# One encoder block on one core: the triangular inversion's rows move to PSUM, the key sums to ScalarE, and other units run beside the inversions

## The chip, the cores and the metric

The kernel runs on one core of a Trainium2 chip. The metric is the device time of one execution in microseconds (us). One execution of each kernel was also taken by the hardware profiler; all rows of a trace shown here are from such an execution.

The engines by their names in the profile: PE is TensorE's matmuls and PEld its weight loads, DVE is VectorE, ACT is ScalarE, POOL is GpSimd, SP is SyncE, which here only issues transfers.

## What is computed

One layer of an encoder for 512 positions and 1024 channels, all in float32:

```python
h = rmsnorm(x, norm1_w)
p, q, k, v, z, bf, bb, af, ab, g_pool, g_dn = split(h @ w_in)
y_pool = (multiscale_pool(p) @ pool_w * pool_scale) @ pool_out      # 4 window widths
q, k, v = split(silu(dwconv_centered([q, k, v], qkv_conv_w)))       # 5 taps along positions
q, k = l2norm(q) * 128 ** -0.5, l2norm(k)                           # 8 heads of 128 channels
o = delta(q, k, v, g_f, beta_f) + flip(delta(flip(q), flip(k), flip(v), flip(g_b), flip(beta_b)))
y_dn = (rmsnorm(o) * dn_norm_w * silu(z)) @ dn_out
x = x + (sigmoid(g_pool) * y_pool + sigmoid(g_dn) * y_dn) @ w_o
u = dwconv_centered(rmsnorm(x, norm2_w) @ ffn_up, ffn_conv_w, ffn_conv_b)
x = x + (silu(u_gate) * u_val) @ ffn_down
return rmsnorm(x, final_norm_w)
```

`delta` is the chunked gated delta rule: within a chunk it solves a system with the matrix I + L, where L is strictly lower triangular and holds the masked and decayed products of the chunk's keys. The kernel inverts such matrices instead.

## The kernel before

**Projections.** Every projection is a `job` (line 405): for 128 output channels and all 512 positions it multiplies 8 blocks of the contraction, each by three matmuls of 128x512 (`mm3`, lines 367 to 370), since weights and activations are split into a high and a low part. A job's weights are loaded raw (`wr_`, SP), cast to the high part by ScalarE (`wh_`, line 392) and subtracted to the low part by GpSimd (`wl_`, line 396). Its result is in a PSUM bank named `ps_`.

**What the units do behind it.** A q, k or v unit runs the convolution: ScalarE does the centre tap (line 736), VectorE four more taps that read PSUM (line 742), ScalarE the activation (752 for v, 754 for q and k). A z unit and a gate unit (`gd`, `gp`) need one ScalarE operation and a store to DRAM. A k unit goes on (`k_unit`): it transposes the keys to token order (line 766, `pt_k`), copies them (`ktok`), squares the other order (`ksq`, line 790), sums the squares by four matmuls with a column of ones (`kss`, line 795) and derives scales from them (798 to 802).

**The inversion.** There are two groups of four heads. For each head `mats_unit` multiplies the keys with themselves (the Gram products `pk`, line 830) and masks them (`nm`, line 837), and stores the 32x32 blocks on the diagonal to DRAM. `inv_unit` then loads a group's 128 blocks, one per partition and 1024 elements each, into SBUF (`rw`, and `un`, half of which ScalarE fills transposed, line 880). In 30 steps VectorE forms an outer product (`tmp`, line 887) and adds it to the rows below (`un`, line 891), both 30 to 240 elements per partition. Then ScalarE writes a transposed copy (`rv`, line 909) and four transfers bring `un` and `rv` to DRAM, from where `ext` is loaded. `merge_unit` builds the 64x64 inverses from there by matmuls (`l1a`, line 951, is the first), and `delta_unit` runs the recurrence for two heads, `fin_unit` normalises and gates the output.

**What sets the order.** The program calls the units one after the other (lines 1404 to 1461), and each adds tasks with an engine, a price in us, what it reads and writes, and a key. The `Planner` (lines 38 to 184) then lays them out in time by these prices: an engine that is free takes the ready task with the lowest key, when a buffer of its ring is free. The outcome is a fixed queue for each engine, worked off strictly in order. Keys of jobs count up in the order of the calls, so this order says which projection fills TensorE beside which chain. The rings (`RINGS`, line 242) are the numbers of buffers, with `oo` the two PSUM banks of the recurrence's output.

Beside the first inversion stand q and v of heads 0 and 1 and k of heads 4 to 7; beside the second q and v of heads 4 to 7 and z of 4 to 7. The gates `gd` come with the merges and recurrences.

Of the kernel before, what the change touches and what calls it, by code (L numbers as in the profile page):

```python
# [208 lines left out]
def hybrid_block(  # L209
# [561 lines left out]
    def k_unit(h, halves=False):  # L771
# [14 lines left out]
        b = {}  # L786

        def square():
            b["sq"] = ring("dp", "f", (P, S), F32, f"ksq_{h}")
            act.activation(b["sq"], kT[h], AF.Square)  # L790

        def sums():
            b["ps"] = bank("ds", f"kss_{h}")
            for t in range(NT):
                pe.matmul(b["ps"][:, t : t + 1], b["sq"][:, t * P : (t + 1) * P], ones[:, 0:1], start=True, stop=True)

        def norm():
            dve.tensor_scalar(out=kss[:, h, :], in0=b["ps"][:, 0:4], scalar1=L2_EPS, scalar2=None, op0=ALU.add)
# [57 lines left out]
    def inv_unit(g):  # L856
        c = CHAIN + 1000 * g + 400
        b = {}
        ui = CHAIN + 1000 * g + 500 - 1e6 * 0
# [4 lines left out]
        fl = lambda t_: t_.rearrange("u r c -> u (r c)")  # L864

        def open_un():
            b["un"] = ring("dp", "x4", (P, B32, B32), F32, f"un_{g}")

        Z(open_un, r=["pool:dp"], w=[f"x4:un{g}"], key=c)

        def load(d):
            if d == 0:
                b["rw"] = ring("dp", "x4", (P, B32, B32), F32, f"rw_{g}")
                sp.dma_start(fl(b["rw"][0:64]), blocks(b_scr[g], 0))
            else:
                sp.dma_start(fl(b["un"][64:128]), blocks(b_scr[g], 1))

        L(256, lambda: load(0), r=[f"bscr{g}", "pool:dp"], w=[f"x4:rw{g}"], key=c)
        L(256, lambda: load(1), r=[f"bscr{g}", "pool:dp"], w=[f"x4:un{g}#b"], key=c)
        A(1.1, lambda: act.copy(b["un"][0:64], b["rw"][0:64].rearrange("p r c -> p c r")),  # L880
          r=[f"x4:rw{g}"], w=[f"x4:un{g}#a"], key=c)

        def step(k):
            un = b["un"]
            n = B32 - 1 - k
# [1 line left out]
            dve.tensor_tensor(  # L887
                out=tm, in0=un[:, k + 1 :, k : k + 1].to_broadcast([P, n, k]),
                in1=un[:, k : k + 1, 0:k].to_broadcast([P, n, k]), op=ALU.mult,
            )  # L890
            dve.tensor_tensor(out=un[:, k + 1 :, 0:k], in0=un[:, k + 1 :, 0:k], in1=tm, op=ALU.add)  # L891
# [12 lines left out]

        V(0.1, end, w=[f"x4:un{g}"], key=c)

        def flip():
# [1 line left out]
            act.copy(b["rv"], b["un"].rearrange("p r c -> p c r"))
# [908 lines left out]
```

## Time and profile before

| what | us |
|---|---|
| median of 3 runs (971.36 to 973.51) | 972.35 |
| the profiled execution | 971.58 |
| its span, first to last recorded instruction | 969.9 |

The page cuts the span into 40 slices of 24.2 us. Each digit is the busy share of a slice in tenths, and PEclk is TensorE's granted clock in tenths of full speed:

```profile
PE   6999969999987889999999999999999999999997
DVE  4787994356689514457213514444344434400302
ACT  5586435244752322444344433444434444421323
POOL 3335234134753421558546860444444545444460
PEclk9999889999998989999999999999999999999999
```

Two places in the first half are less busy on PE (slice 6, and slices 12 to 15), and PEclk is lower there too. The page also follows the chain that ended last back from the last instruction, by engine:

```profile
PE 80%; DVE 12%; ACT 3%; DMA 2%; issue 2%; SPq 1%; POOL 1%; DVEq 0%; POOLq 0%; ACTq 0%
```

In the prediction, a row "start, duration, engine, line, operation, out<-in" is from the timeline, and `[8.52 <-DVE kss L798]` there is the engine's idle time before it and the instruction that ended it. A table of stretches gives for each engine the busy time and the number of instructions in that stretch, then the granted clock and the share of the DMA engines.

### The profile page before, as it was taken

The numbers are of one execution on the slowest core, as the hardware profiler recorded it, in microseconds if no ns is written. First come the engines' busy times: TensorE is split into PE (matmuls) and PEld (weight loads), VectorE is DVE, ScalarE is ACT, GpSimd is POOL, SyncE is SP. The second block draws the span as 40 slices with busy tenths as digits, with TensorE's granted clock in tenths as the row PEclk, the third lists the DMA queues.
The fourth block names the chain that finished last, engine by engine and source line by source line (L and its number), as shares of the span: only waits on it lengthen the run. The fifth ranks groups of instructions, "written<-read, shape, count | busy, mean of one in ns | idle before, by whom it ended". The sixth has DMA issues, their size and how long they took to land.

```text
span 969.9 us, 13976 instructions
## 1 busy us (share of the span) xinstructions
PE 924.5 (95%) x5362; PEld 772.7 (80%) x5362; DVE 457.8 (47%) x860; ACT 411.2 (42%) x646; POOL 428.5 (44%) x415
## 2 busy tenths in 40 slices
PE   6999969999987889999999999999999999999997
PEld 5878757888875669887788888888888888888886
DVE  4787994356689514457213514444344434400302
ACT  5586435244752322444344433444434444421323
POOL 3335234134753421558546860444444545444460
PEclk9999889999998989999999999999999999999999
DMA  6224225323332361323388740233323333222322
GB/s 203 77 72 102 66 73 126 86 77 87 99 91 62 96 167 34 112 65 103 97 268 299 267 152 2 88 107 88 109 87 107 88 104 92 97 100 90 107 87 87
DMA packets 162036, 104.76 MB, mean 108 GB/s; under 512 B 31365, under 2 KB 142770, under 8 KB 161970
## 3 DMA queue, kind: packets, MB, share of 16 engines
q1 hardware_dynamic: 161394, 102.82, 36.3%
q8 instruction: 42, 0.69, 0.3%
q10 hardware_dynamic: 576, 1.05, 0.3%
q14 instruction: 24, 0.20, 0.1%
HBM read 90.22 MB, written 13.63 MB: 107 GB/s over the span
## 4 chain that ended last, share of the span: by engine, by line
PE 80%; DVE 12%; ACT 3%; DMA 2%; issue 2%; SPq 1%; POOL 1%; DVEq 0%; POOLq 0%; ACTq 0%
PE ps_up L369 8%; PE ps_up L370 8%; PE ps_up L368 8%; PE dn L369 4%; PE dn L368 4%; PE dn L370 4%; DVE tmp L887 3%; DVE un L891 3%; PE ps_gd L368 2%; PE ps_z L368 2%; PE o L1164 2%; PE ps_wo L370 2%; PE ps_wo L368 2%; PE ps_wo L369 2%; PE ps_do L368 2%
## 5 line engine op out<-in xcount | busy, mean ns | idle before, releaser
L396 POOL TENSOR_TENSOR wl_up<-wr_up,wh_up 128x512 fp32r<-128x512 f32 x88 | 111.8, 1291 | 156.0 <-ACT wh_up L392 155.9
L369 PE MATMUL ps_up<-h_lo,wh_up 128*128 128x512 f32 (+1 forms) x368 | 139.9, 380 | 0.3 <-DVE h_lo L542 0.3
L368 PE MATMUL ps_up<-h_hi,wh_up 128*128 128x512 f32 (+1 forms) x368 | 140.0, 380 | 0.0
L370 PE MATMUL ps_up<-h_hi,wl_up 128*128 128x512 f32 (+1 forms) x368 | 139.8, 380 | 0.0
L1618 DVE SCALAR_TENSOR_TENSOR c<-ps_up,fw,c 128x511 f32<-128x511 f32 x88 | 66.0, 750 | 122.5 <-ACT c L1612 116.7
L369 PEld LDWEIGHTS ps_up<-h_lo,wh_up 128*128 128x128 f32 x368 | 69.2, 188 | 13.8 <-DVE h_lo L542 0.5
L368 PEld LDWEIGHTS ps_up<-h_hi,wh_up 128*128 128x128 f32 x368 | 69.2, 188 | 13.3
L370 PEld LDWEIGHTS ps_up<-h_hi,wl_up 128*128 128x128 f32 x368 | 69.2, 188 | 12.9
L396 POOL TENSOR_TENSOR wl_dn<-wr_dn,wh_dn 128x512 fp32r<-128x512 f32 x36 | 46.3, 1306 | 49.8 <-ACT wh_dn L392 49.8
L392 ACT CAST wh_up<-wr_up 128x1024 fp32r<-128x1024 f32 x44 | 46.3, 1053 | 47.5 <-PE ps_up L369 37.7
L369 PE MATMUL dn<-wl_dn,a 128*128 128x512 f32 (+1 forms) x158 | 58.6, 371 | 0.0
L368 PE MATMUL dn<-wh_dn,a 128*128 128x512 f32 (+1 forms) x158 | 58.6, 371 | 0.0
L370 PE MATMUL dn<-wh_dn,a 128*128 128x512 f32 (+1 forms) x158 | 58.5, 370 | 0.0
L1677 DVE TENSOR_TENSOR x<-dn,x 128x512 f32<-128x512 f32 (+1 forms) x9 | 5.7, 632 | 96.2 <-PE dn L370 96.1
L396 POOL TENSOR_TENSOR wl_gd<-wr_gd,wh_gd 128x512 fp32r<-128x512 f32 x16 | 20.2, 1281 | 64.7 <-ACT wh_gd L392 31.4
L392 ACT CAST wh_dn<-wr_dn 128x1024 fp32r<-128x1024 f32 x18 | 18.9, 1050 | 61.9 <-PE dn L370 60.1
L1640 ACT CAST a<-c 128x512 fp32r<-128x512 f32 x22 | 13.7, 621 | 53.8 <-DVE c L1636 53.8
L396 POOL TENSOR_TENSOR wl_q<-wr_q,wh_q 128x512 fp32r<-128x512 f32 x16 | 20.7, 1315 | 34.6 <-ACT wh_q L392 34.6
L368 PEld LDWEIGHTS dn<-wh_dn,a 128*128 128x128 f32 x158 | 29.8, 188 | 5.3
L370 PEld LDWEIGHTS dn<-wh_dn,a 128*128 128x128 f32 x158 | 29.7, 188 | 5.2
L369 PEld LDWEIGHTS dn<-wl_dn,a 128*128 128x128 f32 x158 | 29.8, 188 | 5.1
L1612 ACT ACTIVATE c<-ps_up,fw 128x512 f32<-128x512 f32 x44 | 33.8, 768 | 0.0
(334 smaller groups left out, 2410.7 us busy)
## 6 DMA issues: line engine op xcount, KB each, us to landing
wr_up<-in_ffn_up_dram SPq DMA_DIRECT2D x44, 512.0 KB, 3.9
wr_dn<-in_ffn_down_dram SPq DMA_DIRECT2D x22, 512.0 KB, 3.5
x<-in_x_dram SPq DMA_DIRECT2D x8, 512.0 KB, 7.5
wr_k<-in_w_in_dram SPq DMA_DIRECT2D x8, 512.0 KB, 4.0
wr_q<-in_w_in_dram SPq DMA_DIRECT2D x8, 512.0 KB, 4.0
wr_v<-in_w_in_dram SPq DMA_DIRECT2D x8, 512.0 KB, 3.8
wr_z<-in_w_in_dram SPq DMA_DIRECT2D x8, 512.0 KB, 3.9
wr_gd<-in_w_in_dram SPq DMA_DIRECT2D x8, 512.0 KB, 6.2
```

The source lines that it names most:

```text
L368: pe.matmul(ps, ahi, bhi, start=first, stop=False)
L369: pe.matmul(ps, ahi, blo, start=False, stop=False)
L370: pe.matmul(ps, alo, bhi, start=False, stop=last)
L392: act.copy(b["hi"], b["raw"])
L396: pool.tensor_tensor(out=b["lo"][:, sl], in0=b["raw"][:, sl], in1=f32(b["hi"][:, sl]), op=ALU.subtract)
L887: dve.tensor_tensor(out=tm, in0=un[:, k + 1 :, k : k + 1].to_broadcast([P, n, k]), in1=un[:, k : k + 1, 0:k].to_broadcast([P, n, k]), op=A ...
L891: dve.tensor_tensor(out=un[:, k + 1 :, 0:k], in0=un[:, k + 1 :, 0:k], in1=tm, op=ALU.add)
L1164: pe.matmul(o_ps[hh][:, ts(t)], st["w1"][:, s % 2, c, :], dts[hh][:, d, t, :], start=(s == 0 and d == 0), stop=(s == 3 and d == 1),)
L1612: act.activation(b[j], box["ps"], AF.Identity, scale=fw[:, 1, ci : ci + 1], bias=fw[:, 3, ci : ci + 1])
L1618: dve.scalar_tensor_tensor(out=y[:, lo:hi], in0=box["ps"][:, lo + sh : hi + sh], scalar=fw[:, k, ci : ci + 1], in1=y[:, lo:hi], op0=ALU.mu ...
L1640: act.copy(a_hl[c][:, 0, :], b[0])
L1677: dve.tensor_tensor(out=x2[t][:, c0:c1], in0=acc[hf, t, i][:, 0 : c1 - c0], in1=x2[t][:, c0:c1], op=ALU.add)
```

## The change

It has five parts.

1. `inv_unit`: the rows that the steps change, `un`, lie in PSUM, in one tile of two banks (`banks2`; the ring `oo` is now one such tile, which the recurrence's outputs use later). The input block `n` stays in SBUF as one factor of the outer product. ScalarE copies `n` to `un` (`take`) and, at the end, `un` back to SBUF twice, straight (`inv`) and transposed (`rev`), for the four stores.
2. `k_unit`: the squares and their sums are formed by ScalarE in one operation for each of a head's four token blocks, with its accumulator (`accum_out`), from `ktok`; the squares themselves go into the bank of the transposes. The squaring of `kT`, the four matmuls and a PSUM bank go.
3. The prices of GpSimd's copies and of the inversion's steps in the planner.
4. The order of units: beside the first inversion run z of all heads, q and v of heads 0 to 3 and four gates; beside the second q and v of heads 4 to 7, four gates `gd` and three `gp`. The keys of heads 4 to 7 come after the first recurrence. The pool units `p` and the other `gp` come beside the last recurrences.
5. Names in tasks that go with these (`oo`, the bank pairs of the last projection).

```diff
 def cp(n):
-    return 0.25 + n * 0.0024
+    return 0.17 + n * 0.0023
...
-        "pp": 3, "ds": 3, "oo": 2, "raw": 3, "whi": 2, "wlo": 2, "y": 5, "f": 5, "z": 2, "q": 4, "v": 4,
+        "pp": 3, "ds": 3, "oo": 1, "raw": 3, "whi": 2, "wlo": 2, "y": 5, "f": 5, "z": 2, "q": 4, "v": 4,
...
+
+    def banks2(name, shape=(P, 2, 512)):
+        return psum.tile(list(shape), F32, tag="oo", bufs=RINGS["oo"], name=name)
...
-        b = {}
-
-        def square():
-            b["sq"] = ring("dp", "f", (P, S), F32, f"ksq_{h}")
-            act.activation(b["sq"], kT[h], AF.Square)
-
         def sums():
-            b["ps"] = bank("ds", f"kss_{h}")
             for t in range(NT):
-                pe.matmul(b["ps"][:, t : t + 1], b["sq"][:, t * P : (t + 1) * P], ones[:, 0:1], start=True, stop=True)
+                act.activation(
+                    tb["pt"][:, t * P : (t + 1) * P], ktok[h][:, t, :], AF.Square, accum_out=kss[:, h, t : t + 1]
+                )
 
         def norm():
-            dve.tensor_scalar(out=kss[:, h, :], in0=b["ps"][:, 0:4], scalar1=L2_EPS, scalar2=None, op0=ALU.add)
+            dve.tensor_scalar(out=kss[:, h, :], in0=kss[:, h, :], scalar1=L2_EPS, scalar2=None, op0=ALU.add)
             dve.reciprocal(rk2[:, h, :], kss[:, h, :])
             for d in range(2):
                 dve.tensor_tensor(out=bp[:, :, h, d], in0=beta[:, :, h, d], in1=rk2[:, h, rev(d)], op=ALU.mult)
             dve.tensor_scalar(out=nbp[:, :, h, :], in0=bp[:, :, h, :], scalar1=-1.0, scalar2=None, op0=ALU.mult)
 
-        A(ca(512), square, r=[f"kT{h}", "pool:dp"], w=[f"f:ksq{h}"], key=c)
-        M(0.5, sums, r=[f"f:ksq{h}"], w=[f"ds:kss{h}"], key=c)
-        V(0.45, norm, r=[f"ds:kss{h}", "beta"], w=[f"ks{h}"], key=c)
         A(ca(512), keep, r=[tn], w=[f"kk{h}"], key=c)
+        A(2.2, sums, r=[f"kk{h}"], w=[tn, f"ks{h}"], key=c)
+        V(0.85, norm, r=["beta"], w=[f"ks{h}"], key=c)
...
+        Z(lambda: b.update(n=block("n")), r=["pool:dp"], w=[f"x4:n{g}"], key=c)
+        Z(lambda: b.update(rw=block("rw")), r=["pool:dp"], w=[f"x4:rw{g}"], key=c)
+        L(256, lambda: sp.dma_start(fl(b["rw"][lo_]), blocks(b_scr[g], 0)), r=[f"bscr{g}"], w=[f"x4:rw{g}"], key=c)
+        L(256, lambda: sp.dma_start(fl(b["n"][hi_]), blocks(b_scr[g], 1)), r=[f"bscr{g}"], w=[f"x4:n{g}#1"], key=c)
+        A(1.1, lambda: act.copy(b["n"][lo_], b["rw"][lo_].rearrange("p r c -> p c r")),
+          r=[f"x4:rw{g}"], w=[f"x4:n{g}#0"], key=c)
+
+        def take():
+            b["un"] = banks2(f"un_{g}", (P, B32, B32))
+            act.copy(b["un"], b["n"])
+
+        A(1.1, take, r=[f"x4:n{g}"], w=[f"oo:un{g}"], key=c)
...
         def step(k):
             un = b["un"]
             n = B32 - 1 - k
+            if k == 1:
+                b["tmp"] = ring("dp", "x2", (P, 256), F32, f"tmp_{g}")
             tm = b["tmp"][:, 0 : n * k].rearrange("p (r c) -> p r c", c=k)
             dve.tensor_tensor(
-                out=tm, in0=un[:, k + 1 :, k : k + 1].to_broadcast([P, n, k]),
+                out=tm, in0=b["n"][:, k + 1 :, k : k + 1].to_broadcast([P, n, k]),
                 in1=un[:, k : k + 1, 0:k].to_broadcast([P, n, k]), op=ALU.mult,
             )
             dve.tensor_tensor(out=un[:, k + 1 :, 0:k], in0=un[:, k + 1 :, 0:k], in1=tm, op=ALU.add)
 
...
-        def first(k):
-            b["tmp"] = ring("dp", "x2", (P, 256), F32, f"tmp_{g}")
-            step(k)
-
         for k in range(1, B32 - 1):
-            V(0.16 + 2 * (B32 - 1 - k) * k / 960.0, lambda k=k: (first if k == 1 else step)(k),
-              r=[], w=[f"x4:un{g}", f"x2:tmp{g}"], key=c)
+            V(0.44 + 2 * 0.00105 * (B32 - 1 - k) * k, lambda k=k: step(k),
+              r=[f"x4:n{g}"], w=[f"oo:un{g}", f"x2:tmp{g}"], key=c)
 
         def end():
-            un = b["un"]
-            dve.memset(un.rearrange("p r c -> p (r c)")[:, 0 : B32 * B32 : B32 + 1], 1.0)
...
-        V(0.1, end, w=[f"x4:un{g}"], key=c)
-
-        def flip():
-            b["rv"] = ring("dp", "x4", (P, B32, B32), F32, f"rv_{g}")
-            act.copy(b["rv"], b["un"].rearrange("p r c -> p c r"))
-
-        A(1.1, flip, r=[f"x4:un{g}"], w=[f"x4:rv{g}"], key=c)
-        hi_, lo_ = slice(64, 128), slice(0, 64)
-        L(256, lambda: sp.dma_start(blocks(u_scr[g], 1), fl(b["un"][hi_])), r=[f"x4:un{g}"], w=[f"uscr{g}#1"], key=c)
-        L(256, lambda: sp.dma_start(blocks(e_scr[g], 0), fl(b["un"][lo_])), r=[f"x4:un{g}"], w=[f"escr{g}#0"], key=c)
-        L(256, lambda: sp.dma_start(blocks(u_scr[g], 0), fl(b["rv"][lo_])), r=[f"x4:rv{g}"], w=[f"uscr{g}#0"], key=c)
-        L(256, lambda: sp.dma_start(blocks(e_scr[g], 1), fl(b["rv"][hi_])), r=[f"x4:rv{g}"], w=[f"escr{g}#1"], key=c)
+            dve.memset(fl(b["un"])[:, 0 : B32 * B32 : B32 + 1], 1.0)
+
+        V(0.2, end, w=[f"oo:un{g}"], key=c)
+
+        def back(n):
+            b[n] = block(n)
+            act.copy(b[n], b["un"] if n == "inv" else b["un"].rearrange("p r c -> p c r"))
+
+        for n in ("inv", "rev"):
+            A(1.1, lambda n=n: back(n), r=[f"oo:un{g}"], w=[f"x4:{n}{g}"], key=c)
+        for n, rows, scr, d in (("inv", hi_, "u", 1), ("inv", lo_, "e", 0), ("rev", lo_, "u", 0), ("rev", hi_, "e", 1)):
+            dst = u_scr if scr == "u" else e_scr
+            L(256, lambda n=n, rows=rows, dst=dst, d=d: sp.dma_start(blocks(dst[g], d), fl(b[n][rows])),
+              r=[f"x4:{n}{g}"], w=[f"{scr}scr{g}#{d}"], key=c)
...
+                M(FOUR, qs, r=[Sn(s - 1)] + [f"qe:{h}" for h in pair], w=[f"oo:{h0}"], key=c0 + 20)
...
+                    o = banks2(f"o_{h0}")
+                    for i, hh in enumerate(pair):
+                        o_ps[hh] = o[:, i, :]
...
         mats_unit(h)
     k_root(0)
     inv_unit(0)
-    for h in (0, 1):
-        q_unit(h)
-        v_unit(h)
-    for h in range(HG, H):
-        k_unit(h)
-    k_root(1)
-    for h in (2, 3):
-        q_unit(h)
-        v_unit(h)
+
+    def fill(names):
+        for n in names.split():
+            i = int(n[-1])
+            {"z": z_unit, "q": q_unit, "v": v_unit, "k": k_unit, "p": p_unit,
+             "d": lambda c: gate_unit_m("gd", c), "g": lambda c: gate_unit_m("gp", c)}[n[0]](i)
+
+    fill("z0 z1 q0 z2 v0 z3 q1 z4 v1 z5 q2 z6 v2 z7 q3 d0 v3 d1 d2 d3")
...
-    for h in range(4):
-        z_unit(h)
-    gate_unit_m("gd", 0)
...
-    for c in range(1, 4):
-        gate_unit_m("gd", c)
+    fill("k4 k5 k6 k7")
+    k_root(1)
     delta_unit(2)
     fin_unit(2)
     fin_unit(3)
...
     inv_unit(1)
-    for h in range(HG, H):
-        q_unit(h)
-        v_unit(h)
-    for h in range(4, 8):
-        z_unit(h)
+    fill("q4 d4 v4 d5 q5 d6 v5 d7 q6 g0 v6 g1 q7 g2 v7")
     for h in range(HG, H):
         merge_unit(h)
-    for c in range(4, 8):
-        gate_unit_m("gd", c)
     delta_unit(4)
     fin_unit(4)
...
-    for c in range(KD):
-        if c < 4:
-            p_unit(3 - c)
-        gate_unit_m("gp", c)
+    fill("p3 g3 p2 g4 p1 g5 p0 g6 g7")
     for c in range(KD):
```

How this moves instructions. Line numbers are those of each kernel, and numbers behind the names are buffers. First, VectorE within the first inversion, before: the steps, and taps of a k unit.

```order
L887 TENSOR_TENSOR tmp_1176<-un_385 128x198
L891 TENSOR_TENSOR un_385<-un_385,tmp_1176 128x22x9
L742 SCALAR_TENSOR_TENSOR cv_k_1215<-ps_k_1138,cw,cv_k_1215 128x510
L742 SCALAR_TENSOR_TENSOR cv_k_1215<-ps_k_1138,cw,cv_k_1215 128x511 x2
L742 SCALAR_TENSOR_TENSOR cv_k_1215<-ps_k_1138,cw,cv_k_1215 128x510
L887 TENSOR_TENSOR tmp_1176<-un_385 128x210
L891 TENSOR_TENSOR un_385<-un_385,tmp_1176 128x21x10
L887 TENSOR_TENSOR tmp_1176<-un_385 128x220
```

VectorE at the same steps now, where `n` is the block in SBUF and `un` the one in PSUM:

```order
L884 TENSOR_TENSOR tmp_1225<-n_385,un_1213 128x210
L888 TENSOR_TENSOR un_1213<-un_1213,tmp_1225 128x21x10
L884 TENSOR_TENSOR tmp_1225<-n_385,un_1213 128x220
L888 TENSOR_TENSOR un_1213<-un_1213,tmp_1225 128x20x11
L745 SCALAR_TENSOR_TENSOR cv_v_1293<-ps_v_1218,cw,cv_v_1293 128x510
L745 SCALAR_TENSOR_TENSOR cv_v_1293<-ps_v_1218,cw,cv_v_1293 128x511 x2
L745 SCALAR_TENSOR_TENSOR cv_v_1293<-ps_v_1218,cw,cv_v_1293 128x510
L884 TENSOR_TENSOR tmp_1225<-n_385,un_1213 128x228
L888 TENSOR_TENSOR un_1213<-un_1213,tmp_1225 128x19x12
```

The taps between the steps are those of a v unit; between the first and the last step four groups of taps stood before, and two stand now. Next, ScalarE around the end of the first inversion, before (`rv` is the transposed copy):

```order
L736 ACTIVATE cv_k_1343<-ps_k_1258,cw 128x512
L784 COPY ktok_1351<-pt_k_1333 128x512
L754 ACTIVATE kT_1384<-cv_k_1343 128x512
L392 CAST wh_q_1392<-wr_q_1243 128x1024
L736 ACTIVATE cv_q_1405<-ps_q_1324,cw 128x512
L790 ACTIVATE ksq_1410<-kT_1384 128x512
L1210 ACTIVATE oq_0_1418<-qT_882 128x512
L392 CAST wh_v_1442<-wr_v_1307 128x1024
L736 ACTIVATE cv_v_1454<-ps_v_1386,cw 128x512
L909 COPY rv_1469<-un_385 128x1024
L754 ACTIVATE qT_1487<-cv_q_1405 128x512
L784 COPY ktok_1496<-pt_k_1481 128x512
```

And ScalarE at this place now (`inv` and `rev` are the two copies out of PSUM; `zo` is the output of a z unit):

```order
L395 CAST wh_z_1330<-wr_z_1210 128x1024
L1173 ACTIVATE zo_1345<-ps_z_1281 128x512
L1061 ACTIVATE v_1351<-pt_v_1338,rki 128x128 x4
L395 CAST wh_v_1387<-wr_v_1265 128x1024
L739 ACTIVATE cv_q_1397<-ps_q_1326,cw 128x512
L395 CAST wh_z_1431<-wr_z_1317 128x1024
L1173 ACTIVATE zo_1439<-ps_z_1383 128x512
L757 ACTIVATE qT_1447<-cv_q_1397 128x512
L395 CAST wh_q_1493<-wr_q_1373 128x1024
L739 ACTIVATE cv_v_1501<-ps_v_1427,cw 128x512
L901 COPY inv_1508<-un_1213 128x1024
L901 COPY rev_1519<-un_1213 128x1024
```

Ahead of the copy stood the keys of a k unit, their squares and their transposes; now casts, z outputs and a q and a v unit stand there. Last, ScalarE at the start of the second inversion, before (`un` is the copy that opens it):

```order
L1256 CAST o_hi_2842<-ob_2666 128x512
L880 COPY un_2518<-rw_2808 64x1024
L1069 ACTIVATE v_2855<-pt_v_2833,rki 128x128 x4
L392 CAST wh_v_2878<-wr_v_2735 128x1024
L736 ACTIVATE cv_v_2892<-ps_v_2817,cw 128x512
L754 ACTIVATE qT_2900<-cv_q_2831 128x512
L752 ACTIVATE cv_v_2892<-cv_v_2892 128x512
L392 CAST wh_q_2942<-wr_q_2803 128x1024
L736 ACTIVATE cv_q_2954<-ps_q_2874,cw 128x512
L1069 ACTIVATE v_2962<-pt_v_2947,rki 128x128 x4
L754 ACTIVATE qT_2994<-cv_q_2954 128x512
L392 CAST wh_v_3002<-wr_v_2866 128x1024
```

And now (`sgd` and `sgp` are outputs of gates):

```order
L395 CAST wh_q_3115<-wr_q_2967 128x1024
L739 ACTIVATE cv_v_3121<-ps_v_3060,cw 128x512
L869 COPY n_2447<-rw_2465 64x1024
L874 COPY un_3137<-n_2447 128x1024
L755 ACTIVATE cv_v_3121<-cv_v_3121 128x512
L395 CAST wh_gp_3162<-wr_gp_3035 128x1024
L1185 COPY sgd_3177<-ps_gd_3111 128x512
L1061 ACTIVATE v_3185<-pt_v_3172,rki 128x128 x4
L395 CAST wh_v_3223<-wr_v_3103 128x1024
L739 ACTIVATE cv_q_3231<-ps_q_3156,cw 128x512
L395 CAST wh_gp_3265<-wr_gp_3146 128x1024
L1185 COPY sgp_3275<-ps_gp_3219 128x512
```

Casts and taps of q and v alone followed the opening copy; now the copy into PSUM is added, and every second unit is a gate, with one operation and no taps.

More of the change, by code (lines that the diff above doesn't have):

```diff
@@ L858, in inv_unit @@
         b = {}
-        ui = CHAIN + 1000 * g + 500 - 1e6 * 0
+        fl = lambda t_: t_.rearrange("u r c -> u (r c)")
+        hi_, lo_ = slice(64, 128), slice(0, 64)
+        block = lambda n: ring("dp", "x4", (P, B32, B32), F32, f"{n}_{g}")
         def blocks(scr, d):
             return scr.rearrange("b h d t r c -> d (b h) t (r c)")[d]
[L864 to L881, printed above, removed]
+        Z(lambda: b.update(n=block("n")), r=["pool:dp"], w=[f"x4:n{g}"], key=c)
[8 more added lines that the diff above has]
+        A(1.1, take, r=[f"x4:n{g}"], w=[f"oo:un{g}"], key=c)
         def step(k):
@@ L1121, in delta_unit @@
                 V(4 * cd(128), resid, r=[f"ds:ks{h0}{s}", "neg_eg"] + [f"v:{h}" for h in pair], w=[Rn], key=c0)
-                M(FOUR, qs, r=[Sn(s - 1)] + [f"qe:{h}" for h in pair], w=[f"oo:{h}" for h in pair], key=c0 + 20)
+                M(FOUR, qs, r=[Sn(s - 1)] + [f"qe:{h}" for h in pair], w=[f"oo:{h0}"], key=c0 + 20)
             def solve(s=s, ch=ch, b=b):
@@ L1160, in attn @@
                 if s == 0:
-                    for hh in pair:
-                        o_ps[hh] = bank("oo", f"o_{hh}")
+                    o = banks2(f"o_{h0}")
+                    for i, hh in enumerate(pair):
+                        o_ps[hh] = o[:, i, :]
                 for c, (hh, d, t) in enumerate(ch):
@@ L1167, in attn @@
                     )
-            M(FOUR, attn, r=[w1n(s)] + [f"r4:dt{h}" for h in pair], w=[f"oo:{h}" for h in pair], key=c0 + 21)
+            M(FOUR, attn, r=[w1n(s)] + [f"r4:dt{h}" for h in pair], w=[f"oo:{h0}"], key=c0 + 21)
     o_hl = [None] * H
@@ L1222, in fin_unit @@
         A(ca(512), q2, r=[f"q:{h}"], w=[n("a")], key=c)
-        A(ca(512), take, r=[f"oo:{h}"], w=[n("o")], key=c)
+        A(ca(512), take, r=[f"oo:{h - h % 2}"], w=[n("o")], key=c)
         A(ca(512), square, r=[n("o")], w=[n("sq")], key=c)
@@ L1344, in pmap @@
             mm3(b["p2"], b["w"][:, 0], b["w"][:, 1], b["yhi"], b["ylo"], True, True)
-        M(MM3, pmap, r=[f"pwr:{g}", f"y:yh{g}", f"y:yl{g}"], w=[f"ds:pw{g}"], key=u)
+        M(MM3, pmap, r=[f"pwr:{g}", f"y:yh{g}", f"y:yl{g}"], w=[f"ds:pw{g}", f"r4:pm{g}"], key=u)
         def sc_hi():
@@ L1661, in accn @@
         tag = "oo" if cut(hf, t) > 1 else "pp" if t < 2 else "ds"
-        return tag, f"{tag}:dn{hf}{t}{i}"
+        return tag, f"{tag}:dn{hf}{t}#{i}"
     def dmm(hf, k, t, i):
@@ L1666, in dmm @@
         if (hf, t, i) not in acc:
-            acc[hf, t, i] = bank(accn(hf, t, i)[0], f"dn_{hf}_{t}{i}")
+            if cut(hf, t) > 1:
+                both = banks2(f"dn_{hf}_{t}")
+                for j in range(2):
+                    acc[hf, t, j] = both[:, j, :]
+            else:
+                acc[hf, t, i] = bank(accn(hf, t, i)[0], f"dn_{hf}_{t}")
         ts_, cs = slice(t * P, (t + 1) * P), slice(i * w, (i + 1) * w)
```

## The prediction

> **What bounds the kernel now.** I read the page first, then the busy time stage by stage, then the waits, and last the rows of the two inversions.
>
> ```profile
> span 969.9 us, 13976 instructions
> ...
> PE 924.5 (95%) x5362; PEld 772.7 (80%) x5362; DVE 457.8 (47%) x860; ACT 411.2 (42%) x646; POOL 428.5 (44%) x415
> ...
> core 0: us, PE busy (x) PEld busy (x) DVE busy (x) ACT busy (x) POOL busy (x), PEclk, DMA share, GB/s
> 37.00:94.00 57.00, 55.89 (x291) 44.70 (x291) 48.39 (x128) 40.38 (x64) 22.36 (x22) 1.00 0.31 77
> 94.00:156.00 62.00, 52.13 (x259) 42.91 (x258) 53.65 (x111) 28.14 (x44) 21.13 (x20) 0.86 0.33 84
> 186.00:276.00 90.00, 90.00 (x540) 77.54 (x537) 54.78 (x141) 48.43 (x76) 40.94 (x32) 1.00 0.31 85
> 276.00:338.00 62.00, 49.12 (x204) 39.49 (x203) 50.59 (x83) 19.20 (x33) 25.14 (x20) 0.89 0.28 75
> 351.00:375.00 24.00, 19.29 (x303) 16.79 (x302) 6.91 (x18) 7.34 (x18) 2.98 (x3) 0.86 0.39 97
> 480.00:492.00 12.00, 12.00 (x54) 9.93 (x53) 0.00 (x0) 2.74 (x5) 4.36 (x6) 1.00 0.50 161
> ```
>
> TensorE is the bound: 95% busy, and wholly busy from 186 to 276 us. The rest is lost in three places. There TensorE stands idle, and the granted clock falls, so that its matmuls take longer. I count both: idle time, plus one minus the clock times the busy time. The first inversion (94 to 156) loses 62 − 52.13 = 9.9 idle and 0.14 × 52.13 = 7.3 by the clock, 17.2 us. The second (276 to 338) loses 12.9 + 0.11 × 49.12 = 18.3, and the stage of 351 to 375 loses 4.7 + 0.14 × 19.29 = 7.4. Together 42.9 us. Where nothing is lost, a 128x512 matmul costs 12.00 / 54 = 0.222 us.
>
> Why TensorE starves beside an inversion shows on VectorE, which does the inversion's 30 steps (two operations each) and, between them, the convolution taps of the q, k and v units. It is busy for 53.65 of 62 and 50.59 of 62 us there.
>
> ```profile
> L891 DVE TENSOR_TENSOR un<-un,tmp 128x30 f32<-128x30 f32 (+14 forms) x60 | 31.8, 530 | 2.1
> L887 DVE TENSOR_TENSOR tmp<-un 128x30 f32<-128x30 f32 (+14 forms) x60 | 31.8, 529 | 1.8
> ...
> 98.28 0.21 DVE L887 TENSOR_TENSOR tmp<-un 128x30 f32<-128x30 f32 x1
> 98.52 0.22 DVE L891 TENSOR_TENSOR un<-un,tmp 128x30 f32<-128x30 f32 x1
> 100.45 0.29 DVE L887 TENSOR_TENSOR tmp<-un 128x130 f32<-128x130 f32 x1
> 100.78 1.27 DVE L891 TENSOR_TENSOR un<-un,tmp 128x130 f32<-128x130 f32 x1
> 102.08 1.28 DVE L887 TENSOR_TENSOR tmp<-un 128x150 f32<-128x150 f32 x1
> 118.05 0.40 DVE L887 TENSOR_TENSOR tmp<-un 128x240 f32<-128x240 f32 x1
> 118.48 0.41 DVE L891 TENSOR_TENSOR un<-un,tmp 128x240 f32<-128x240 f32 x1
> 100.62 2.58 POOL L396 TENSOR_TENSOR wl_k<-wr_k,wh_k 128x512 fp32r<-128x512 f32 x2 [3.50 <-PE pt_k L766]
> L742 DVE SCALAR_TENSOR_TENSOR cv_v<-ps_v,cw,cv_v x32: 735/749/752, 72.9 to 324.2; 128x510 f32<-128x510 f32 x16, 128x511 f32<-128x511 f32 x16
> L1055 DVE TENSOR_TENSOR dt<-pkq,dt x16: 653/681/692, 80.2 to 328.2; 128x512 f32<-128x512 f32 x16
> 105.94 3.10 DVE L742 SCALAR_TENSOR_TENSOR cv_k<-ps_k,cw,cv_k 128x510 f32<-128x510 f32 x4
> ```
>
> A step's operation takes 0.21 to 0.41 us, but the two that meet the POOL subtraction at 100.62 take 1.27 and 1.28: these operations, all in SBUF, are held up while GpSimd runs. The taps (L742) and L1055, which have an operand in PSUM, keep to 735 to 752 and 653 to 692 ns all through both inversions, POOL busy or not. That contrast is what the change uses.
>
> **The change part by part.**
>
> **Key norms.** Today each head squares its transposed keys and sums them by four small matmuls.
>
> ```profile
> 49.37 0.79 PE kss L795 x8
> 42.69 0.62 ACT L790 ACTIVATE ksq<-kT 128x512 f32<-128x512 f32 x1
> L512 ACT ACTIVATION_READ_ACCUMULATOR sq<-x x4: 186/192/199, 578.0 to 602.9; 128x1 f32 x4
> 39.42 1.28 ACT L754 ACT_TABLE_LOAD   x1
> 40.71 0.63 ACT L754 ACTIVATE kT<-cv_k 128x512 f32<-128x512 f32 x1
> ```
>
> The row is one head: eight heads take 8 × 0.79 = **6.3 us off TensorE**. ScalarE gets instead 32 squares of 128 columns with accumulator, about 0.29 each (a quarter of the columns of a 0.62 operation, with some start-up) and 0.19 for each accumulator read, 15 us, and loses 8 × 0.62 = 5. The built program holds 28 table loads against 20, 8 × 1.28 = 10.3 us. With the four added copies of an inversion's block (about 1.05 each, 4.2) ScalarE gains some 24.5 us, in a kernel where it is busy 42%. It is crowded only where k units stand together: 40.38 of 57 us from 37 to 94, before anything is added. I take 3 us for that, bounds 0 (TensorE has other units ready) and 10 (all the added sums and loads of the four late units show: 24.5 × 4/8, less the copies).
>
> [...]
>
> **The step's price in PSUM.** No row before has such a step: the second operation reads and writes PSUM, the first reads one operand there. Start to start, today's undisturbed operations take 0.24 (30 elements) to 0.43 (240). With 165 elements on average that is 0.36, and 60 operations make 21.7 us an inversion, my value: PSUM rows show no surcharge to speak of (L1055, 512 elements, 0.681; the SBUF pair, carried on at the slope of 0.19 us for 210 elements, comes to 0.66). Upper bound 0.08 more each, 26.5 us. The lower bound leaves out the gaps between operations: the mean of 0.21 and 0.41, 0.31 × 60 = 18.6. Today an inversion's steps take 31.8 us, of which 10 are hold-ups by POOL in the first and 14.5 in the second.
>
> [...]
>
> **First inversion.** What must now pass while TensorE eats its fill:
>
> ```profile
> 80.02 1.95 PE L830 MATMUL pk<-kT 128*128 128x128 f32 x16
> 83.84 4.22 DVE L837 SCALAR_TENSOR_TENSOR nm<-pk,nbp,dt 128x128 f32<-128x128 f32 x16
> 96.09 2.15 ACT L880 COPY un<-rw 64x1024 f32<-64x1024 f32 x1
> 141.53 1.96 ACT L909 COPY rv<-un 128x1024 f32<-128x1024 f32 x1 [8.52 <-DVE kss L798]
> 155.31 0.45 PE L951 MATMUL l1a<-ext,nm 32*32 32x32 f32 x32
> ```
>
> In the order of the changed program 252 matmuls and 20 transposes stand on TensorE between the last Gram product and the first merge: 272 × 0.222 = 60.4 us. The chain beside it: the last head's masks, half of 4.22, 2.2; from their end (88.06) to the first step (98.28), over two transfers and the flip, 10.2; the new copy into PSUM 1.05; steps 21.7; two groups of four taps between them (four today), 2 × 3.05; one copy more at the end 1.05; and from the steps' end (141.4) to the first merge (155.31) 13.9. Sum 56.2, **4.2 less than the fill**. So TensorE should not wait. The fill also feeds more easily: z and gate units need one ScalarE operation and no taps. Today the flip at 141.53 had stood 8.52 us behind a k unit's activation in ScalarE's queue; the fill now has no k units. I keep 2 us of the 17.2 as lost.
>
> **Second inversion.**
>
> ```profile
> 261.42 2.15 DVE L837 SCALAR_TENSOR_TENSOR nm<-pk,nbp,dt 128x128 f32<-128x128 f32 x8
> 274.75 0.35 DVE L887 TENSOR_TENSOR tmp<-un 128x30 f32<-128x30 f32 x1
> 325.05 0.19 DVE L891 TENSOR_TENSOR un<-un,tmp 128x30 f32<-128x30 f32 x1
> 338.13 0.45 PE L951 MATMUL l1a<-ext,nm 32*32 32x32 f32 x32
> ```
>
> The fill is 255 matmuls and 28 transposes, 62.8 us. The chain is 2.2 for the masks, 11.2 (263.57 to 274.75), 1.05, steps and two tap groups 27.8, 1.05, and 12.9 (325.24 to 338.13): 56.2. With one tap group that stands ahead of the masks, 3.05, it makes 59.3. Slack 3.5; I keep 2 of the 18.3 as lost.
>
> **The stage of 351 to 375.** Here the merges wait for the loads of `ext`, queued on SP behind a gate's weights and a z load:
>
> ```profile
> 346.24 4.33 SPq L384 DMA_DIRECT2D wr_gd<-in_w_in_dram  x3
> 350.67 1.64 SPq L1206 DMA_DIRECT2D zs<-z_scr  x1
> 352.40 5.21 SPq L937 DMA_DIRECT2D ext<-e_scr  x8
> ```
>
> The change moves those gates into the fill, so a part of the queue goes; the z load stays. I let 4 of 7.4 remain, bounds 0 and 7.4.
>
> **Moved work.** Gates and z units keep their matmuls and DMAs; they only change places, at no cost while TensorE is busy on either side. The late k4 to k7 stand in a stage like 186 to 276, where TensorE has never waited and VectorE (54.78 of 90) and ScalarE (48.43) have room. The pool units go beside the recurrences:
>
> ```profile
> L1290 DVE TENSOR_TENSOR pool_s<-pool_s 128x525 f32<-128x525 f32 (+2 forms) x6 | 7.1, 1187 | 0.3
> ```
>
> The recurrence's own VectorE operations queue behind these. I take 2 us, bounds 0 and 7.1.
>
> **Sum.** 971.6 (the profiled execution) − 6.3 − 15.2 − 16.3 − 3.4 + 3 + 2 = 935.4. The runs' median lies 0.8 above the profiled execution: **936 us**. Against it the unknown terms can move: crowding −3 to +7, the pool units −2 to +5.1, the ext stage −4 to +3.4, the 4 us kept as lost −4 to 0, and the steps 0 to +1.9 (4.8 each at the upper bound, less the slacks 4.2 and 3.5). All at one end would be 923 or 953; since they hardly all go one way, the forecast's own range is 924 to 948.
>
> **The rivals.**
> (A) The hold-up stays: POOL delays PSUM steps as it delays SBUF ones, the second operand `n` and `tmp` being in SBUF. Then the chains are 10 and 14.5 longer, less the slacks 4.2 and 3.5, 17 us: 953. For it: L887 reads `n` in SBUF. Against: L742 and L1055 read an SBUF operand too and are never held. Chance 0.08.
> (B) ScalarE becomes the bound where k units stand together: their sums, 1.9 us a head, and a table load delay the activations of the next units, and TensorE waits for them. Gives back half to four fifths of ScalarE's added 24.5, 12 to 20: 948 to 956. For it: 40.38 of 57 already. [...] Chance 0.14.
> (C) Slower: a PSUM step is dear, because the broadcast, the short rows or the write to PSUM cost more than any row shows. The inversion is a chain, so each 0.1 us an operation costs 6 us an inversion once the slack is gone. The change is then lost when both chains grow by what was won, about 36 us over two, after some 8 of slack: 44 / 120 = 0.37 above 0.36. From **0.73 to 0.77 us** an operation it is slower than before; at 1.0, 60 × 0.64 − 4 = 34 each, 936 + 69 = 1005. Against: the 512-element PSUM rows at 0.68 with three times the elements. Chance 0.07.
> (D) The wait only moves: the same TensorE idle time appears at the merges or in the k stage, and just the 6.3 us of sums remain: 965; half of this lies within 0.2%. Chance 0.06.
> Better than 924 (all losses vanish and nothing crowds): 0.05. The forecast has 0.60.
>
> The range 921 to 955 takes in A and most of B; it leaves out C, D and the far ends, under 0.2. Chances: faster by over 0.2% (2 us, about what a measurement of this kernel can tell) 0.90; within, 0.03 (half of D); slower, C, 0.07.
>
> **What will show it.** Right: step operations of 0.25 to 0.5 us without any above 0.8, also under a POOL subtraction; TensorE busy over 95% with clock 1.0 from the last Gram to the first merge, twice; no rows kss on TensorE; table loads of 1.28 on ScalarE. Wrong: steps of 0.7 or more; waits of TensorE for ScalarE's keys and values in the late k stage; a hold of the recurrence behind pool_s; `ext` loads still late.

## The result, and the profile after

| | us |
|---|---|
| before, median of 4 runs | 971.89 |
| changed, median of 4 runs (933.10 to 935.24) | **933.85** |
| ratio to before, 95% interval | 0.9607 (0.9590 to 0.9625) |
| the profiled execution of the changed kernel, and its span | 934.32, 932.6 |

The change makes the kernel 3.9% faster; 936 was forecast, with 921 to 955 as the range. The page of the changed kernel has these busy rows:

```profile
span 932.6 us, 13916 instructions
...
PE 905.5 (97%) x5298; PEld 757.6 (81%) x5298; DVE 434.9 (47%) x860; ACT 432.9 (46%) x714; POOL 427.6 (46%) x415
```

TensorE's idle time, span less busy, fell from 969.9 − 924.5 = 45.4 to 27.1 us, and its busy time by 19.0, to which the 64 records fewer of the key sums and the better clock (0.991 against 0.978) both belong. The table of stretches, cut at the changed kernel's own stages (columns as before: length, five engines, granted clock, transfers):

```profile
94.00:151.00 57.00, 57.00 (x266) 47.24 (x264) 37.53 (x87) 26.29 (x40) 29.32 (x24) 1.00 0.49 135
151.00:187.00 36.00, 30.84 (x559) 25.54 (x559) 13.69 (x33) 12.93 (x35) 8.53 (x14) 0.91 0.40 89
187.00:288.00 101.00, 101.00 (x568) 85.42 (x566) 62.97 (x156) 65.39 (x118) 48.38 (x41) 1.00 0.32 86
288.00:350.00 62.00, 62.00 (x293) 51.57 (x291) 43.48 (x99) 30.36 (x47) 33.58 (x30) 1.00 0.49 130
350.00:374.00 24.00, 20.36 (x406) 15.73 (x405) 11.04 (x23) 10.23 (x28) 7.64 (x11) 0.93 0.53 112
...
424.00:468.00 44.00, 43.14 (x213) 35.86 (x212) 18.57 (x28) 24.82 (x40) 26.49 (x28) 1.00 0.44 142
```

Beside both inversions (94 to 151, 288 to 350) TensorE is now wholly busy at full clock: the 17.2 and 18.3 us that were lost there are gone. The stretch with the late keys (187 to 288) is wholly busy as well, although ScalarE works 65.39 of its 101 us. What is left is lost at the merges. By the same count as before, idle plus one minus the clock times busy: 151 to 187 loses 5.2 + 0.09 × 30.84 = 7.9 us, 350 to 374 loses 3.6 + 0.07 × 20.36 = 5.1. The list of waits and one row of the timeline name what TensorE waits for:

```profile
PE l1a L943 <- DMA ext<-e_scr: 8.1, 5, 4.4
```

```profile
168.60 1.02 PE L943 MATMUL l1a<-ext,nm 32*32 32x32 f32 x32 [4.36 <-DMA ext<-e_scr]
```

TensorE's queue comes to the merges before the inverted blocks are back from DRAM. The transfers issued on SP just ahead show what stands before them:

```profile
159.16 1.14 SPq L387 DMA_DIRECT2D wr_gd<-in_w_in_dram  x2
160.40 1.01 SPq L387 DMA_DIRECT2D wr_k<-in_w_in_dram  x1
161.51 7.10 SPq L929 DMA_DIRECT2D ext<-e_scr  x8
```

Three weight loads of 512 KB each go out directly ahead of the `ext` loads of the third and fourth head. From 161 to 167 us the DMA engines are wholly busy and move 275 GB/s (112 over the whole span), and these `ext` loads take 4.6 to 5.3 us from issue to landing; those of the first two heads, issued from 147 on, took 1.8 to 2.0. The second group has the same picture from 357 to 366, with two `gp` loads and one `p` load ahead: the DMA engines are busy 96% and move 209 GB/s, and the `ext` loads take 2.5 to 3.8 us. No run moves these weights away, so what that would bring is not shown.

The steps themselves are as the timeline of VectorE and GpSimd shows (start, duration, operation):

```profile
107.58 0.24 DVE L884 TENSOR_TENSOR tmp<-n,un 128x84 f32<-128x84 f32 x1
107.86 0.25 DVE L888 TENSOR_TENSOR un<-un,tmp 128x84 f32<-128x84 f32 x1
108.15 0.27 DVE L884 TENSOR_TENSOR tmp<-n,un 128x108 f32<-128x108 f32 x1
108.45 0.28 DVE L888 TENSOR_TENSOR un<-un,tmp 128x108 f32<-128x108 f32 x1
...
134.16 0.20 DVE L888 TENSOR_TENSOR un<-un,tmp 128x30 f32<-128x30 f32 x1
...
107.62 2.54 POOL L399 TENSOR_TENSOR wl_z<-wr_z,wh_z 128x512 fp32r<-128x512 f32 x2 [4.01 <-ACT wh_z L395]
```

GpSimd subtracts from 107.62 to 110.16, and the steps beside it keep their 0.24 to 0.28 us. The groups (busy, mean ns) show the same for all 120 operations: 19.6 and 20.3 us where it was 31.8 and 31.8.

```profile
L888 DVE TENSOR_TENSOR un<-un,tmp 128x30 f32<-128x30 f32 (+14 forms) x60 | 20.3, 338 | 2.1
...
L884 DVE TENSOR_TENSOR tmp<-n,un 128x30 f32<-128x30 f32 (+14 forms) x60 | 19.6, 327 | 3.7 <-ACT un L874 1.9
```

### The profile page after: what moved, and what is told of

Its sections match the earlier page's. It is cut to its first block, busy times and chain, and to the rows that moved or that the text cites. A ratio compares the mean times of both kernels' runs of the same rounds, so it can differ in the third digit from the quotient of the medians.

```text
span 932.6 us, 13916 instructions
## 1 busy us (share of the span) xinstructions
PE 905.5 (97%) x5298; PEld 757.6 (81%) x5298; DVE 434.9 (47%) x860; ACT 432.9 (46%) x714; POOL 427.6 (46%) x415
## 4 chain that ended last, share of the span: by engine, by line
PE 86%; DMA 5%; DVE 3%; SPq 2%; issue 1%; POOL 1%; ACT 1%; DVEq 0%; POOLq 0%; ACTq 0%
PE ps_up L372 9%; PE ps_up L373 9%; PE ps_up L371 9%; PE dn L371 4%; PE dn L372 4%; PE dn L373 4%; PE pw L1120 2%; PE o L1157 2%; DMA ext<-e_scr 2%; PE ps_wo L373 2%; PE ps_wo L371 2%; PE ps_wo L372 2%; PE ps_do L372 2%; PE ps_do L373 2%; PE ps_do L371 2%; PE ps_gd L371 1%
## 5 line engine op out<-in xcount | busy, mean ns | idle before, releaser
L399 POOL TENSOR_TENSOR wl_z<-wr_z,wh_z 128x512 fp32r<-128x512 f32 x16 | 20.3, 1290 | 32.0 <-ACT wh_z L395 32.0
```

The source lines that it names most:

```text
L399: pool.tensor_tensor(out=b["lo"][:, sl], in0=b["raw"][:, sl], in1=f32(b["hi"][:, sl]), op=ALU.subtract)
```

## The experiments

Ten kernels undo a part of the changed kernel or put one part, or two, into the kernel before; two more try to go further. The medians come from three batches, in which the kernel before had 971.12, 972.59 and 971.68, so a difference of 1.5 us between kernels of different batches need not be one of the kernels. The changed kernel was not run in them again; its 933.85 is from the result.

### Where the rows lie

**inv_in_sbuf.** The changed kernel with `un` in SBUF; all five queues hold the same instructions in the same order.

```diff
-            b["un"] = banks2(f"un_{g}", (P, B32, B32))
+            b["un"] = block("un")
```

> The changed kernel with the inversion's rows in SBUF again; every queue has the same instructions in the same order, only the place of un differs. Theory (operations all in SBUF are held up by GpSimd's subtractions): step operations of 1.0 to 1.4 us come back, some 8 to 16 in each inversion, all of them beside a GpSimd subtraction; the steps take 8 to 14 us longer, and the time is 939 to 958. Rival (the new neighbours did it, not the place): no step operation above 0.5 us, time within 2 of 933.9.

Measured: 952.11 us (ratio 0.9803, 0.9780 to 0.9826), 18 us more than the changed kernel. The same place in its timeline:

```profile
107.38 0.24 DVE L884 TENSOR_TENSOR tmp<-n,un 128x84 f32<-128x84 f32 x1
107.66 1.23 DVE L888 TENSOR_TENSOR un<-un,tmp 128x84 f32<-128x84 f32 x1
108.92 1.22 DVE L884 TENSOR_TENSOR tmp<-n,un 128x108 f32<-128x108 f32 x1
110.18 0.97 DVE L888 TENSOR_TENSOR un<-un,tmp 128x108 f32<-128x108 f32 x1
...
107.38 2.64 POOL L399 TENSOR_TENSOR wl_z<-wr_z,wh_z 128x512 fp32r<-128x512 f32 x2 [3.76 <-ACT wh_z L395]
```

The same operations beside the same subtraction take 1.23 and 1.22 in place of 0.25 and 0.27. In all, the two lines are busy for 31.5 and 31.2 us, 22.8 more than in PSUM. The rival (the neighbours, not the place) falls.

**tmp_in_psum.** The rows in SBUF and only the product `tmp` in PSUM; again the same queues.

```diff
-            b["un"] = banks2(f"un_{g}", (P, B32, B32))
+            b["un"] = block("un")
...
-                b["tmp"] = ring("dp", "x2", (P, 256), F32, f"tmp_{g}")
+                b["tmp"] = banks2(f"tmp_{g}")[:, 0, 0:256]
```

> The changed kernel with the rows in SBUF and the product tmp in PSUM, so that each step operation has one operand in PSUM: the first only its output (both inputs in SBUF), the second one input. Same instructions in the same order. Theory (any PSUM operand frees the operation): no step operation above 0.5 us, time 932 to 936. Rival (both inputs in SBUF are enough to be held): the first operation of a step shows 1.0 to 1.4 us beside GpSimd, the second does not; half of the hold-ups, time 936 to 948.

Measured: 943.45 (0.9705, 0.9689 to 0.9722), about half way. The same place:

```profile
107.42 1.39 DVE L884 TENSOR_TENSOR tmp<-n,un 128x84 f32<-128x84 f32 x1
108.85 0.24 DVE L888 TENSOR_TENSOR un<-un,tmp 128x84 f32<-128x84 f32 x1
109.12 0.95 DVE L884 TENSOR_TENSOR tmp<-n,un 128x108 f32<-128x108 f32 x1
110.11 0.27 DVE L888 TENSOR_TENSOR un<-un,tmp 128x108 f32<-128x108 f32 x1
...
107.40 2.53 POOL L399 TENSOR_TENSOR wl_z<-wr_z,wh_z 128x512 fp32r<-128x512 f32 x2 [3.72 <-ACT wh_z L395]
```

Only the first operation of a step is held, the one with both inputs in SBUF and its output in PSUM. The second, with one input in PSUM and its output in SBUF, never is (0.41 us at most, of 60). My theory (any operand in PSUM) falls to the rival: it is the **inputs** that count here. That the changed kernel has no slow step is so because both of its operations read `un`.

### The key norms

**norms_on_pe** is the changed kernel with the squares and matmuls of before, **norms_alone** the kernel before with only the new norms. The edit is that of `k_unit` in the change, undone and done; a part of it:

```diff
         def sums():
-            for t in range(NT):
-                act.activation(
-                    tb["pt"][:, t * P : (t + 1) * P], ktok[h][:, t, :], AF.Square, accum_out=kss[:, h, t : t + 1]
-                )
+            b["ps"] = bank("ds", f"kss_{h}")
+            for t in range(NT):
+                pe.matmul(b["ps"][:, t : t + 1], b["sq"][:, t * P : (t + 1) * P], ones[:, 0:1], start=True, stop=True)
```

> The changed kernel with the key norms by the squares and matmuls of before. Theory (6.3 us of matmuls off a busy TensorE, ScalarE has room): 938 to 942. Rival (the sums crowd ScalarE and cost as much as they bring): 930 to 936.

Measured: 941.16 (0.9691, 0.9676 to 0.9707), 7.3 above the changed kernel, as the theory had it.

> The kernel before with only the new key norms. Theory (they take matmuls off TensorE also where it is the bound): 962 to 967. Rival (where the inversion is the bound the saved matmuls only lengthen the waits, and ScalarE is later): 969 to 975.

Measured: 969.96 (0.9965, 0.9950 to 0.9980), a gain of 2.6, at the fast end of what the rival gave. The page says where the rest stayed:

```profile
span 968.3 us, 13899 instructions
...
PE 916.1 (95%) x5298; PEld 765.2 (79%) x5298; DVE 452.9 (47%) x860; ACT 423.1 (44%) x704; POOL 426.5 (44%) x415
```

TensorE is busy 8.4 us less than before (924.5) and idle 52.2 us against 45.4. So 6.8 of the 8.4 us saved turned into waiting here, where the inversions are the bound; in the changed kernel, where TensorE is, the norms bring 7.3. In both runs the planner also laid the queues out anew (TensorE's longest waits stand elsewhere in norms_alone than before), so a part of the 2.6 and of the 7.3 can be order; this was not separated.

### The order of units

**old_order** is the changed kernel with the calls of before, **order_alone** the kernel before with the new calls:

```diff
-    fill("z0 z1 q0 z2 v0 z3 q1 z4 v1 z5 q2 z6 v2 z7 q3 d0 v3 d1 d2 d3")
+    for h in (0, 1):
+        q_unit(h)
+        v_unit(h)
+    for h in range(HG, H):
+        k_unit(h)
...
```

> The changed kernel with the order of units of before: k4 to k7 and q, v beside the first inversion, z and gates later. Theory (the order carries a good part: taps and k units between the steps): the steps are quick but four and five tap groups stand between them, TensorE waits beside the inversions are about halved, 944 to 956. Rival (the PSUM rows carry all): 933 to 938.

Measured: 931.74 (0.9590, 0.9575 to 0.9604). This is below both expectations. The interval overlaps that of the changed kernel (0.9590 to 0.9625): the order of before is not worse, and 2.1 us better by the medians, which is not clear of noise. The theory falls.

> The kernel before with only the new order of units (rows in SBUF, norms by matmuls, prices of before). Theory (the new order and the PSUM rows cure the same waits, so the order is worth something only while the steps are held up): 971 less the 19 of the SBUF run, plus the 7 of the norms, 956 to 964. Rival (the order is worth nothing in any kernel): 968 to 974.

Measured: 973.75 (1.0019, 1.0001 to 1.0036). The new order alone wins nothing either, and this theory falls too. In this kernel TensorE has its longest wait behind a step sequence that is still held up (VectorE and then TensorE):

```profile
316.89 1.22 DVE L891 TENSOR_TENSOR un<-un,tmp 128x58 f32<-128x58 f32 x1
...
332.40 3.10 DVE L742 SCALAR_TENSOR_TENSOR cv_v<-ps_v,cw,cv_v 128x510 f32<-128x510 f32 x4
...
336.27 1.12 PE L766 MATMUL pt_v<-ident,cv_v 128*128 128x128 f32 x4 [9.76 <-ACT cv_v L752]
```

The taps of v stand behind the first half of the steps, which the planner, by its prices, took to be over sooner than they were.

### The prices, which the prediction had left out

**old_step_price** is the changed kernel with one line undone; **prices_alone**, **rows_alone** and **psum_alone** put the prices (of steps and GpSimd copies), the rows, or both, into the kernel before.

```diff
-            V(0.44 + 2 * 0.00105 * (B32 - 1 - k) * k, lambda k=k: step(k),
+            V(0.16 + 2 * (B32 - 1 - k) * k / 960.0, lambda k=k: step(k),
```

> The changed kernel with the step price of before in the planner (it lays the steps out at half their time). Theory (a true price matters, since the planner then places what stands behind the steps too early): 937 to 946, with waits of the steps' followers. Rival (with fast steps and a fill without taps the price is no matter): 931 to 936.

Measured: 949.08 (0.9757, 0.9728 to 0.9785), more than the theory gave: **15 us lost by one number that runs nowhere on the chip**. No step is slower: the group of `un` is as quick as in the changed kernel. But the order differs. In the timeline of this kernel, VectorE and then TensorE:

```profile
117.80 0.42 DVE L888 TENSOR_TENSOR un<-un,tmp 128x240 f32<-128x240 f32 x1
118.12 3.09 DVE L745 SCALAR_TENSOR_TENSOR cv_v<-ps_v,cw,cv_v 128x510 f32<-128x510 f32 x4
...
121.99 1.11 PE L769 MATMUL pt_v<-ident,cv_v 128*128 128x128 f32 x4 [3.32 <-ACT cv_v L755]
```

and the same taps in the changed kernel:

```profile
113.68 0.40 DVE L888 TENSOR_TENSOR un<-un,tmp 128x220 f32<-128x220 f32 x1
113.99 3.10 DVE L745 SCALAR_TENSOR_TENSOR cv_v<-ps_v,cw,cv_v 128x510 f32<-128x510 f32 x4
```

With the low price the taps stand behind five more steps (16 in place of 11), and TensorE, whose place in the order was worked out for a VectorE that would be done, waits 3.32 us for them. This is the largest wait that the changed kernel does not have. In all, TensorE is idle 34.5 us here against 27.1, and busy 5.2 longer, at a mean granted clock of 0.987 against 0.991; how the 15 us split over the single waits was not worked out.

> The kernel before with only the new prices in the planner (steps and GpSimd copies); rows in SBUF, order and norms of before. Theory (a step priced at half its time makes the planner put other work too early or too late, which cost 15 in the changed kernel): 953 to 963. Rival (the price helps only where steps keep to it; here they are still held up): 967 to 975.

Measured: 963.28 (0.9924, 0.9907 to 0.9941), at the edge of what the theory gave. The steps are still held up here (maximum 1447 ns), and busy for 69.0 us against 63.6 before; the gain of 8.4 is the planner's alone.

> The kernel before with only the rows in PSUM, at the prices of before. Theory (rows and prices each carry a part): 950 to 960. Rival (the rows carry all, as the steps come close to any price): 939 to 945.

Measured: 951.99 (0.9796, 0.9781 to 0.9811), as the theory had it.

> The kernel before with only the rows in PSUM and the prices that go with them (order of before, norms by matmuls). Theory (the PSUM rows carry most of the gain): old_order plus the 7 of the norms, 936 to 942. Rival (they need the short ScalarE queue of the new norms or order): 945 to 960.

Measured: 941.70 (0.9676, 0.9662 to 0.9691), as the theory had it. Three of these and the kernel before make a square, in the order and with the norms of before:

| us | prices of before | new prices |
|---|---|---|
| rows in SBUF | 971.7 | 963.3 |
| rows in PSUM | 952.0 | 941.7 |

The rows bring 19.7 or 21.6, the prices 8.4 or 10.3: nearly independent. (The 941.7 is from another batch than the rest, with the kernel before 0.9 slower.) The new norms on top lead to old_order's 931.7, another 10, or 8 by the ratios to the kernel before. Which of the two prices matters more was not tried in this square; in the changed kernel the step's alone is worth 15.

### Two attempts at a faster kernel

**ext_three** gives old_order a third buffer for the merges' `ext` (and takes one from ring `f`):

```diff
-        "pp": 3, "ds": 3, "oo": 1, "raw": 3, "whi": 2, "wlo": 2, "y": 5, "f": 5, "z": 2, "q": 4, "v": 4,
-        "r4": 8, "x4": 3, "qe": 4, "ext": 2, "x1": 1, "x2": 1, "xs": 2, "pw": 1, "pwr": 1, "cv3": 4, "fo": 2, "sq2": 1,
+        "pp": 3, "ds": 3, "oo": 1, "raw": 3, "whi": 2, "wlo": 2, "y": 5, "f": 4, "z": 2, "q": 4, "v": 4,
+        "r4": 8, "x4": 3, "qe": 4, "ext": 3, "x1": 1, "x2": 1, "xs": 2, "pw": 1, "pwr": 1, "cv3": 4, "fo": 2, "sq2": 1,
```

> The old_order kernel with three ext buffers in place of two, and four of ring f in place of five, as the room asks. TensorE's longest remaining waits there are the merges' for loads of ext, whose buffers come free only after two merges. Theory (the loads of the third and fourth head start earlier): 926 to 930. Rival (the waits are for the transfers themselves, or ring f is missed): 931 to 936.

Measured: 936.36 (0.9640, 0.9622 to 0.9659), slower than old_order, at the edge of the rival. Its list of waits:

```profile
PE l1a L943 <- DMA ext<-e_scr: 13.0, 4, 5.1
```

The waits for `ext` grew from 6.5 us there to 13.0. The trace shows the loads of the fourth head behind two weight loads again (`wr_q` and `wr_v`, issued at 176.07 and 176.58), from 177.34 on, and TensorE stands 5.15 us for them, until 183.99. How much of the loss is this, the missing `f` or what else the planner did was not separated.

**mixed_order** puts the late keys beside the first inversion again, between z units:

```diff
-    fill("z0 z1 q0 z2 v0 z3 q1 z4 v1 z5 q2 z6 v2 z7 q3 d0 v3 d1 d2 d3")
+    fill("q0 v0 k4 z0 k5 z1 k6 z2 k7 z3")
+    k_root(1)
+    fill("q1 v1 q2 v2 q3 v3 z4 z5 d0")
...
-    fill("k4 k5 k6 k7")
-    k_root(1)
+    fill("z6 z7 d1 d2 d3")
```

> The changed kernel with an order between the two: the keys k4 to k7 beside the first inversion, alternating with z units, q and v 1 to 3 and two more z units behind them. Theory (early keys let the second inversion start early, and z units keep the taps off the steps): 927 to 931. Rival (with fast steps the order is no matter): 931 to 936.

Measured: 937.29 (0.9651, 0.9636 to 0.9665). Neither expectation: slower than both of the orders that it mixes. Its TensorE is idle for 26.8 us, no longer than the changed kernel's 27.1, but busy 4.9 longer, at a mean granted clock of 0.986 against 0.991. Orders that all have quick, truly priced steps thus differ by up to 5.6 us (931.7 to 937.3); which waits and which stretches at a lower clock make this up was not followed further. No run beats old_order, whose median is below those of both kernels.

## Why the prediction came out right, and where it was wrong

**The bound and the steps: right.** The steps in PSUM were put at 21.7 us an inversion, 27.8 with two groups of taps; the first runs from 106.60 to 134.36, which is 27.8, and no operation takes above 0.42. The fill came as forecast too: from the last Gram product to the first merge 60.3 and 62.8 us, against 60.4 and 62.8. The chain took all of it: 56.6 and 57.5 us from the masks to the first merge against 54.0, and in the first inversion the last load for that merge, issued at 149.22, lands 1.8 us later, just as TensorE comes to it at 151.08. It does not wait, but the slack of 4.2 was not there. Of the two errors of the steps that I allowed, (A) and (C), neither came. But the reason given in (A), that L742 and L1055 read an SBUF operand too, covers only operations with a PSUM input; tmp_in_psum shows that a PSUM output alone would have left half of the hold-ups.

In neighbouring rows of one step there, the operation with both inputs in SBUF takes 1.39 us and the one with an input in PSUM 0.24. No run shows the 0.08 us that the upper bound adds to each operation: the second operation of a step measures 0.20 at 30 elements and 0.42 at 240 in PSUM, 0.22 and 0.41 in SBUF.

**The cause of the gain: wrong in part.** The step that failed is "the fill also feeds more easily: z and gate units need one ScalarE operation and no taps", with "two groups of four taps between them (four today)". old_order has its k units beside the first inversion and five groups of taps between the steps, and is not slower. TensorE is well filled there too (9 on the page, 90% or more, in each slice from 93 to 163 us, and idle for 930.4 − 907.6 = 22.8 us in all): it has work enough beside a longer chain once the steps are quick and truly priced. The reading that stood beside this step was wrong as well. I had put ScalarE's 8.52 us before the flip down to a k unit's activation ahead of it in the queue. But that is time in which ScalarE did nothing, and the flip starts at 141.53, where the steps end:

```profile
141.24 0.19 DVE L891 TENSOR_TENSOR un<-un,tmp 128x30 f32<-128x30 f32 x1
141.41 0.09 DVE L903 MEMSET un<- 128x32 f32 x1
```

The flip waited for the steps, not for a k unit.

**The prices: a missing term.** The prediction has no line for them, though the diff shows the number, and 0.50 us (the old mean price of a step) against two operations of 0.36 could have been read off. That is worth 8 to 15 us here. It stands inside the 35 us that I put down to rows and order.

**The merges: undersized.** I left 2 and 2 us as lost beside the inversions and 4 at the second group's merges, 8 in all. Beside the inversions nothing is lost; at the merges 7.9 + 5.1 = 13.0 are, mostly behind loads of `ext`. The 7.9 stand at the first group's merges, where the kernel before lost nothing (30.00 of 30 us busy from 156 to 186, at full clock) and the sum has no term: so much of rival (D), the wait that only moves, did come. The step that failed is "The change moves those gates into the fill, so a part of the queue goes". Other weight loads stand in their place, `gd` and `k` in the first group and `gp` and `p` in the second, as the rows of SP above show. A sign of being wrong that I had named, "`ext` loads still late", showed. A third buffer for the loads (ext_three) did not help.

**Crowding and pool units: oversized.** I took 3 and 2. TensorE is busy 101.00 of 101 us beside the late keys, so 0, and the stretch 424 to 468 loses 0.9 where it lost 2.3. With these in place the sum closes: 971.6 − 6.3 − (42.9 − 13.0) − 1.4 = 934.0, against 934.3 measured. The 936 was so close because an error of +5 at the merges met one of −6.4 here, which is luck. Without it the time would still have lain in the range.

**The norms: right in the changed kernel** (6.3 forecast, 7.3 measured), and rival (B), ScalarE as the bound, did not come. ScalarE's added time is near the estimate of 24.5, 432.9 − 411.2 = 21.7. The eight added table loads are not the norms', though: norms_on_pe has 30, norms_alone 22, against 28 in the changed kernel and 20 before. In the timeline of the changed kernel:

```profile
85.51 0.28 ACT L791 ACTIVATE pt_k<-ktok 128x128 f32<-128x128 f32 x1
85.72 0.19 ACT L791 ACTIVATION_READ_ACCUMULATOR pt_k<-ktok 128x1 f32 x1
...
88.62 0.68 ACT L739 ACTIVATE cv_v<-ps_v,cw 128x512 f32<-128x512 f32 x1
89.32 1.28 ACT L255 ACT_TABLE_LOAD   x1
90.62 0.21 ACT L813 ACTIVATE rki<-kss 128x16 f32<-128x16 f32 x1
```

A sum costs 0.28 + 0.19 as estimated. The table load of 1.28 us starts 0.02 us behind the activation before it, and the next activation 0.02 us behind the load.
